# Gates and branches of a hybrid encoder with the tokens stationary and 512 columns moving, and pool sums on VectorE

## The chip, the cores and the metric

The kernel runs on one core of one Trainium2 chip. The time is the device time of one execution of the whole program in microseconds (us), two layers of the encoder from input to output. Less is better. 0.2 % of it, about 1.7 us, is what a measurement of this kernel can tell from no change.

## The reference

Two layers over 256 tokens of 1024 channels, in float32. Each layer is a mixer with three branches and a gated feed-forward part:

```python
h = rmsnorm(x, norm_mix_pre[l])
proj = jnp.einsum('bsd,de->bse', h, w_in[l])           # 1024 -> 5888
qa, ka, va, pu, qc, kc, vc, gl = jnp.split(proj, splits, axis=-1)
ya = global_axial_attention(qa, ka, va, ...)           # A: 8 heads, 2 kv heads, rope
yb = pool_mixer(pu, w_pool[l], pool_scale[l])          # B: means over 2, 4, 8, 16 tokens, minus u
yc = neighbourhood_attention(qc, kc, vc, rpb[l])       # C: 8 heads, window of the token grid
z = jnp.einsum('bsnc,ncd->bsnd', ys, w_branch[l])      # three times 512 -> 1024
gates = jax.nn.sigmoid(gl + b_gate[l]).reshape(B, S, N_BRANCH, D_MODEL)
mix = jnp.einsum('bsd,de->bse', jnp.sum(gates * z, axis=2), w_out[l])
x = x + rmsnorm(mix, norm_mix_post[l])
f = conv_gated_mlp(rmsnorm(x, norm_ffn_pre[l]), ...)   # w_up 1024 -> 2 x 2816, conv of 3 taps, gelu, w_down
x = x + rmsnorm(f, norm_ffn_post[l])
```

## The kernel before

**Weights.** All weights lie in DRAM as 264 chunks of 512 KB (128 x 1024 float32), 132 to a layer, in the order in which they are used. SP's queue loads them into `raw` (5 buffers). ScalarE (ACT) rounds each half of a chunk to `hi` (`split`, L156), and the rest, `lo` = `raw` - `hi`, is taken by VectorE (DVE), or by GpSimd (POOL) for each chunk whose number leaves 1 by 5 (L157). `hi` and `lo` have 6 buffers each. `feed` splits chunks ahead as buffers come free, at a priority that is put behind the other work's.

**Products.** Every product of the large projections is three matmuls, hi by hi, hi by lo and lo by hi (`mm3`, L193 to L195). `wstat` keeps the weights stationary: a 128 x 128 block of them is loaded and 256 tokens of `hT` (the normed, turned activations) move past it, so a matmul is 256 wide and its result is already turned (channels on partitions). `rows`, and the first projections (q, k, v), keep 128 tokens stationary and move 512 columns of weights; their result has tokens on partitions.

**A layer, in order.**
1. Projections k, v and q of attention A (chunks 0 to 5), and in `prep_a` their norm and rotary turn on DVE, ACT and POOL, one time for each half of the tokens, t = 0 and 1. At its end PE turns the rows, and ACT and DVE write `k2`, `klo` (L393) and `q2` (L397).
2. `pool_u`, four pieces of 128 channels for the pool branch, then eight pieces for q and k of attention C. Among the latter lie attention A's steps (`drive(att)`: `scores` L446 and L447, softmax L449 to L460, `turn` L468) and one step each of `pool_sums`, 12 additions, products and differences on POOL (L573 to L585).
3. v of attention C, 512 wide, whose rows POOL's queue copies into `vb`.
4. Gates and branches: 24 calls of `gated`, for the branches B, A and C in turn, one for each 128 channels d. Each is 12 matmuls of `w_branch` by `y` and 24 of the gate's columns of `w_in`, all 256 wide, into the two halves of one PSUM bank; ACT takes the tanh of the gate with its bias from `bg` (one bias per partition), DVE weighs and adds up. Attention A's end and attention C are driven between them. For branch C each call ends a merged piece, split into hi and lo, and the rows of `w_out` 0 to 2 are issued among the last calls.
5. The rest of `w_out` (`tail`), then `boundary`: `residual`, norm and the turn of `hT` for t = 0 and 1. While it runs, PE has the first two pieces of `w_up` (val and gate), with tokens stationary and 256 wide; they are turned later, in pieces f = 2 and 3.
6. The other 20 pairs of pieces of `w_up` by `wstat`, the convolution of three taps (`conv`, L749 to L751), gelu, and `w_down` three pieces behind (`LAG`), with its own tail and boundary.

**What sets the order.** Each engine runs its instructions in one order that a scheduler fixes when the program is built: it goes by the order in the code, moved by priorities (`urgent` forward, `feed` back). An engine whose next instruction waits does nothing behind it.

## Time and profile before

| | us |
|---|---|
| median of 3 runs | 850.67 (850.04 to 851.77) |
| time of the profiled execution | 851.73 |
| its span, first to last instruction | 850.0 |
| TensorE (PE) busy in it | 817.6, 96 % |
| VectorE (DVE) busy | 584.7, 69 % |
| ScalarE (ACT) busy | 505.0, 59 % |
| GpSimd (POOL) busy | 234.1, 28 % |
| mean granted clock of TensorE | 0.993 of 2.4 GHz |

The profiled execution's own time is 1.73 us over its span and 1.06 us over the median. PE's busy time counts the time from a matmul's start to its modelled end, and matmuls overlap, so the distance from start to start tells more than the duration of one. An x4 at the end of a row is a group of four instructions, and the number in brackets is the idle time before the row's first instruction, with what ended it.

### The profile page before, as it was taken

The page shows a single profiled execution, that of the slowest core. Times are in us where ns is not written, and L with a number is a line of the kernel's source. Part 1 is how long each engine was busy: PE and PEld are TensorE (multiplying, and loading weights), DVE is VectorE, ACT ScalarE, POOL GpSimd, SP SyncE. Part 2 cuts the span into 40 slices and gives each one's busy share as a digit, 9 for nine tenths or more (in the row PEclk, how much of TensorE's full clock was granted, in tenths as well). Part 3 has the DMA queues.
Part 4 walks back from the last instruction along what each step waited for, and adds up shares of the span by engine and source line. Part 5 has one row for each costly group of instructions (what it writes and reads, how often), then busy time and mean ns, then how long its engine had stood idle before and what let it go on. Part 6 is the DMA issues. An engine that isn't in the chain of part 4 may idle for free.

```text
span 850.0 us, 15776 instructions
## 1 busy us (share of the span) xinstructions
PE 817.6 (96%) x6020; PEld 762.0 (90%) x6020; DVE 584.7 (69%) x1084; ACT 505.0 (59%) x1096; POOL 234.1 (28%) x225
## 2 busy tenths in 40 slices
PE   5979999999989999999999999999998999999997
PEld 4878899999989999999988888999997999999995
DVE  4798465565688767676778975655567786676774
ACT  6467566454567656565565775654455765656562
POOL 3675321212123121212144915112122121212120
PEclk9999999999999999999999999999999999999999
DMA  7844556465465756665464555545655565566631
GB/s 272 306 155 170 162 188 209 149 203 170 150 200 170 224 175 198 175 197 175 148 198 151 173 153 170 172 152 168 195 171 165 195 184 191 177 195 181 191 99 49
DMA packets 43291, 151.44 MB, mean 178 GB/s; under 512 B 5968, under 2 KB 6224, under 8 KB 42960
## 3 DMA queue, kind: packets, MB, share of 16 engines
q1 hardware_dynamic: 42192, 148.34, 55.1%
q0 software_dynamic: 1024, 2.10, 0.8%
q8 instruction: 47, 0.77, 0.4%
q14 instruction: 28, 0.23, 0.1%
HBM read 147.27 MB, written 1.05 MB: 175 GB/s over the span
## 4 chain that ended last, share of the span: by engine, by line
PE 84%; DVE 7%; issue 3%; ACT 2%; POOL 1%; DMA 1%; SPq 0%; DVEq 0%; POOLq 0%; ACTq 0%
PE ps L193 27%; PE ps L195 26%; PE ps L194 26%; DVE lo L157 3%; POOL st L212 1%; DMA x<-in_x 1%; DVE big L239 1%; PE ps L478 1%; ACT hi L156 1%; PE ps L468 1%; PE ps L527 1%; PE ps L494 1%; PE ps L244 1%; DVE big L376 0%; DVE x L259 0%
## 5 line engine op out<-in xcount | busy, mean ns | idle before, releaser
L156 ACT ACTIVATE hi<-raw 128x512 fp32r<-128x512 f32 x528 | 315.6, 625 | 180.8 <-PE ps L194 83.6
L157 DVE TENSOR_TENSOR lo<-raw,hi 128x512 fp32r<-128x512 f32 x422 | 308.0, 746 | 115.5 <-ACT hi L156 113.3
L195 PE MATMUL ps<-hThi,lo 128*128 128x256 f32 x1216 | 345.7, 284 | 1.5 <-DVE lo L157 1.5
L193 PE MATMUL ps<-hThi,hi 128*128 128x256 f32 x1216 | 346.3, 285 | 0.0
L194 PE MATMUL ps<-hTlo,hi 128*128 128x256 f32 x1216 | 345.6, 284 | 0.0
L157 POOL TENSOR_TENSOR lo<-raw,hi 128x512 fp32r<-128x512 f32 x106 | 147.5, 1411 | 503.4 <-ACT hi L156 489.5
L193 PEld LDWEIGHTS ps<-hThi,hi 128*128 128x128 f32 x1216 | 234.8, 193 | 2.1 <-issue 0.8
L195 PEld LDWEIGHTS ps<-hThi,lo 128*128 128x128 f32 x1216 | 234.8, 193 | 1.7 <-DVE lo L157 1.7
L194 PEld LDWEIGHTS ps<-hTlo,hi 128*128 128x128 f32 x1216 | 234.7, 193 | 1.3
L749 ACT ACTIVATE w<-ps,cvp 128x256 f32<-128x256 f32 x88 | 48.6, 556 | 38.6 <-DVE w L751 38.6
L193 PE MATMUL ps<-hi,y 128*128 128x512 f32 x176 | 69.1, 393 | 0.1
L194 PE MATMUL ps<-lo,y 128*128 128x512 f32 x176 | 68.9, 392 | 0.0
L195 PE MATMUL ps<-hi,y 128*128 128x512 f32 x176 | 68.5, 389 | 0.0
L750 DVE SCALAR_TENSOR_TENSOR w<-ps,cvp,w 128x255 f32<-128x255 f32 x88 | 42.1, 480 | 34.0 <-ACT w L749 33.8
L193 PE MATMUL ps<-y,hi 128*128 128x256 f32 x192 | 55.8, 290 | 0.0
L195 PE MATMUL ps<-hi,hTlo 128*128 128x256 f32 (+1 forms) x160 | 53.2, 334 | 1.8 <-DVE hTlo L201 1.8
L193 PE MATMUL ps<-hi,hThi 128*128 128x256 f32 (+1 forms) x160 | 54.1, 341 | 0.5 <-ACT hThi L200 0.3
L195 PE MATMUL ps<-y,lo 128*128 128x256 f32 x192 | 54.3, 283 | 0.0
L194 PE MATMUL ps<-y,hi 128*128 128x256 f32 x192 | 54.3, 283 | 0.0
L194 PE MATMUL ps<-lo,hThi 128*128 128x256 f32 (+1 forms) x160 | 53.0, 333 | 0.3 <-POOL lo L157 0.3
L212 POOL TENSOR_TENSOR st<-st,mhalf 128x1 f32<-128x1 f32 (+1 forms) x20 | 20.3, 1013 | 82.6 <-DVE st L222 65.0
L751 DVE SCALAR_TENSOR_TENSOR w<-ps,cvp,w 128x255 f32<-128x255 f32 x88 | 41.9, 479 | 1.0
...
## 6 DMA issues: line engine op xcount, KB each, us to landing
raw<-in_wall SPq DMA_DIRECT2D x264, 512.0 KB, 3.8
...
```

The source lines that it names most:

```text
L156: act.activation(hi[c][:, z], raw[c][:, z], AF.Copy)
L157: (pool if c % PN == 1 else dve).tensor_tensor(lo[c][:, z], raw[c][:, z], hi[c][:, z], op=OP.subtract)
L193: pe.matmul(o, a[0], b[0], start=first, stop=False)
L194: pe.matmul(o, a[0], b[1], start=False, stop=False)
L195: pe.matmul(o, a[1], b[0], start=False, stop=last)
L212: pool.tensor_tensor(r, v, mhalf[:, :width], op=OP.pow)
L239: par["xn"] = dve.scalar_tensor_tensor(xn[:, c], xs[t][:, c], r, g[:, c], op0=OP.mult, op1=OP.mult)
L244: pe.transpose(p[:, 128 * k:128 * k + 128], xn[:, 512 * h + 128 * k:512 * h + 128 * k + 128], ident)
L468: pe.transpose(p3[:, k, t * 128:(t + 1) * 128], e[:, t, k * 128:(k + 1) * 128], ident)
L749: act.activation(u[:, c:c + S], p[:, c:c + S], AF.Identity, bias=cvp[:, l, j, 3:4], scale=cvp[:, l, j, 1:2])
L750: dve.scalar_tensor_tensor(u[:, c + 1:c + S], p[:, c:c + S - 1], cvp[:, l, j, 0:1], u[:, c + 1:c + S], op0=OP.mult, op1=OP.add)
L751: dve.scalar_tensor_tensor(u[:, c:c + S - 1], p[:, c + 1:c + S], cvp[:, l, j, 2:3], u[:, c:c + S - 1], op0=OP.mult, op1=OP.add)
```

## The change

Four things are changed.

- Gates and branches become six steps (i, c) in a layer: a branch i and a half c of its 1024 output channels. A step has 24 matmuls of `w_branch` for each half of the tokens and 48 of the gate's columns, all with tokens stationary and 512 wide, into two `pz` and two `pg` banks. The gate's bias now lies along the row, so it is a tile of its own, `gb`, spread over the partitions by a DMA on SP's queue (12 in the program, two buffers) and added by DVE before the tanh (`weighed`). The merged rows have tokens on partitions and are turned by PE (`turn_merged`, four groups of four transposes in a layer) before ACT and DVE split them. `w_out`'s first rows are issued within the last step, its rows 1 and 2 behind it.
- `pool_sums` runs on DVE in place of POOL.
- The lo of the chunks of `w_in` with columns below 2816 (q, k, v, pool, attention C) is always taken by DVE, so POOL has 44 chunks in place of 53.
- The first four pieces of `w_up`, val and gate, are 512 wide with tokens stationary (`turned`), and are turned in pieces f = 4 to 7; `w_down` follows five pieces behind. The tiles `w1` have 4 buffers in place of 6.

A "..." stands for lines left out.

```diff
 NY = 20
-TAIL_O, TAIL_D, LAG = 5, 6, 3
+TAIL_O, TAIL_D, LAG = 5, 6, 5
...
-                    out.append(("w_branch", l, i, 0, 4, 128 * d, 256))
-                wide("w_in", 0, 2816 + 1024 * i + 128 * d, 128)
-                if i == 2 and 1 <= d <= 8 - TAIL_O:
-                    out.append(("w_out", l, 0, d - 1, 1, 0, 1024))
+            for c in range(2):
+                for k in (0, 2):
+                    out.append(("w_branch", l, i, k, 2, 512 * c, 512))
+                if i == 2 and c == 1:
+                    out.append(("w_out", l, 0, 0, 1, 0, 1024))
+                wide("w_in", 0, 2816 + 1024 * i + 512 * c, 512)
+        for d in range(1, 8 - TAIL_O):
+            out.append(("w_out", l, 0, d, 1, 0, 1024))
         for d in range(8 - TAIL_O, 8):
             out.append(("w_out", l, 0, d, 1, 0, 1024))
-        wide("w_up", 0, 0, 256)
-        wide("w_up", 0, 128 * NF, 256)
-        for f in range(2, NF):
+        wide("w_up", 0, 0, 128 * NT)
+        wide("w_up", 0, 128 * NF, 128 * NT)
+        for f in range(NT, NF):
             wide("w_up", 0, 128 * f, 128)
             wide("w_up", 0, 128 * (NF + f), 128)
             if 0 <= f - LAG < NF - TAIL_D:
...
-        return sb.tile([128, 256], FT, name="w1", bufs=6)
+        return sb.tile([128, 256], FT, name="w1", bufs=4)
...
-        (pool if c % PN == 1 else dve).tensor_tensor(lo[c][:, z], raw[c][:, z], hi[c][:, z], op=OP.subtract)
+
+        lean = c % PN == 1 and (CHUNKS[c][0] != "w_in" or CHUNKS[c][5] >= 2816)
+        (pool if lean else dve).tensor_tensor(lo[c][:, z], raw[c][:, z], hi[c][:, z], op=OP.subtract)
...
-            pool.tensor_tensor(a[:, :, :271], u[:, :, :271], u[:, :, 1:272], op=OP.add)
-            pool.tensor_tensor(b[:, 1:, :269], a[:, 1:, :269], a[:, 1:, 2:271], op=OP.add)
+            dve.tensor_tensor(a[:, :, :271], u[:, :, :271], u[:, :, 1:272], op=OP.add)
+            dve.tensor_tensor(b[:, 1:, :269], a[:, 1:, :269], a[:, 1:, 2:271], op=OP.add)
...
-                pool.tensor_tensor(d, src[:, g, 8 - w // 2:264 - w // 2], invc[:, g], op=OP.mult)
-                pool.tensor_tensor(d, d, u[:, g, 8:264], op=OP.subtract)
+                dve.tensor_tensor(d, src[:, g, 8 - w // 2:264 - w // 2], invc[:, g], op=OP.mult)
+                dve.tensor_tensor(d, d, u[:, g, 8:264], op=OP.subtract)
...
-        acc = [sb.tile([128, 4, S], FT, name="q2", bufs=2) for _ in range(2)]
+        acc = [sb.tile([128, D], FT, name="q2", bufs=2) for _ in range(2)]
...
-        def gated(i, d, y, wz):
-            p = psbank()
-            for c in range(4):
-                mm3(p[:, :S], [wz[z][:, c, 128 * (d % 2):128 * (d % 2) + 128] for z in range(2)], y[c], c == 0, c == 3)
-            if d % 2 == 1:
-                done()
-            wstat(p[:, S:], "w_in")
-            g = w1()
-            act.activation(g, p[:, S:], AF.Tanh, bias=bg[:, l, 8 * i + d:8 * i + d + 1], scale=0.5)
-            a = acc[d // 4][:, d % 4]
-            if i == 1:
-                dve.scalar_tensor_tensor(a, g, 1.0, p[:, :S], op0=OP.add, op1=OP.mult)
-                return
-            m = w1()
-            dve.scalar_tensor_tensor(m, g, 1.0, p[:, :S], op0=OP.add, op1=OP.mult)
-            if i == 0:
-                dve.tensor_tensor(a, a, m, op=OP.add)
-                return
-            dve.tensor_tensor(m, a, m, op=OP.add)
...
-            merged[d] = merged["hi"][:, d], merged["lo"][:, d % 4]
-            act.activation(merged[d][0], m, AF.Copy, scale=0.5)
-            dve.scalar_tensor_tensor(merged[d][1], m, 0.5, merged[d][0].bitcast(FT), op0=OP.mult, op1=OP.subtract)
...
-        for i, y in ((1, yB), (0, yA), (2, yC)):
-            if i == 2:
...
+        def out_rows(d):
+
+            (w,) = take("w_out")
+            for t in range(2):
+                for h in range(2):
+                    rows(ob[t][h], merged[d], t, w, h, d == 0, False)
+            done()
+            feed()
+        def gate_bias(n):
+            i, c = steps[n]
+            g = sb.tile([128, 512], FT, name="gb", bufs=2)
+            nc.sync.dma_start(g, brow(bgate[l, i, 512 * c:512 * c + 512], 512))
+            gbias[n] = g
+        def weighed(i, c, t, pz, pg, gb):
+
+            g, a = w2(), acc[t][:, 512 * c:512 * c + 512]
+            dve.tensor_tensor(g, pg, gb, op=OP.add)
+            act.activation(g, g, AF.Tanh, scale=0.5)
+            if i == 1:
+                dve.scalar_tensor_tensor(a, g, 1.0, pz, op0=OP.add, op1=OP.mult)
+                return
+            dve.scalar_tensor_tensor(g, g, 1.0, pz, op0=OP.add, op1=OP.mult)
+            dve.tensor_tensor(a, a, g, op=OP.add)
...
+        def turn_merged(c, t):
+            p = psbank()
+            for k in range(4):
+                pe.transpose(p[:, 128 * k:128 * k + 128], acc[t][:, 512 * c + 128 * k:512 * c + 128 * k + 128], ident)
...
+            ts = slice(t * 128, (t + 1) * 128)
+            split_from(merged["hi"][:, 4 * c:4 * c + 4, ts], merged["lo", c][:, :, ts], p.rearrange("p (k n) -> p k n", k=4), 0.5)
...
+        steps = [(i, c) for i in (1, 0, 2) for c in range(2)]
...
+        for n, (i, c) in enumerate(steps):
+            if i == 2 and c == 0:
...
+            ws = take("w_branch", 2)
+            pz, pg = [psbank(), psbank()], []
+            for t in range(2):
+                for k in range(4):
+                    w = ws[k // 2]
+                    mm3(pz[t], [y[:, t * 128:(t + 1) * 128] for y in ys[i][k]], [w[0][:, k % 2], w[1][:, k % 2]], k == 0, k == 3)
+                    if t == 1 and k % 2 == 1:
+                        done()
+                        feed()
...
+            if n + 1 < len(steps):
+                gate_bias(n + 1)
+            if i == 2 and c == 1:
+                for t in range(2):
+                    turn_merged(0, t)
+                ob = [[psbank(), psbank()] for _ in range(2)]
+                out_rows(0)
+            ws = take("w_in", 4)
+            for t in range(2):
+                pg.append(psbank())
+                for k in range(8):
+                    w = ws[k // 2]
+                    mm3(pg[t], kx(k, t), [w[0][:, k % 2], w[1][:, k % 2]], k == 0, k == 7)
+                    if t == 1 and k % 2 == 1:
+                        done()
+                        feed()
+                weighed(i, c, t, pz[t], pg[t], gbias[n])
+                if i < 2:
+                    drive(att)
+        for d in range(1, 8 - TAIL_O):
+            if d == 1:
+                turn_merged(1, 0)
+            out_rows(d)
+        turn_merged(1, 1)
...
-        ws = take("w_up", 4)
-        tb = [psbank(), psbank()]
-        tk = [w2(), w2()]
-        for t in range(2):
-            for z in range(2):
-                for k in range(8):
-                    w = ws[2 * z + k // 4]
-                    mm3(tb[t][:, S * z:S * z + S], kx(k, t), [w[0][:, k % 4], w[1][:, k % 4]], k == 0, k == 7)
-                    if k % 4 == 3 and t == 0:
-                        drive(bound[1], z * (k // 7) * 2)
-                    elif k % 4 == 3:
-                        done()
-                        if k < 7 or z == 0:
-                            feed()
-            act.activation(tk[t], tb[t], AF.Copy)
...
+        ws = []
+        tk = [big()[:, :D] for t in range(2)]
...
+        def turned(t, c):
+            z, k = c // 4, 2 * (c % 4)
+            if k == 0:
+                tb[t, z] = psbank()
             if t == 0:
-                for _ in bound[1]:
-                    pass
-        feed()
+                ws.extend(take("w_up"))
+            for i in range(2):
+                mm3(tb[t, z], kx(k + i, t), [ws[c][0][:, i], ws[c][1][:, i]], k + i == 0, k + i == 7)
+            if t == 1:
+                done()
+                feed()
+            if k == 6:
+                act.activation(tk[t][:, 512 * z:512 * z + 512], tb[t, z], AF.Copy)
+
+        for c in range(NSPL):
+            turned(0, c)
+        for _ in bound[1]:
+            pass
+        for c in range(4):
+            turned(1, c)
+        for c in range(NSPL, 8):
+            turned(0, c)
+        for c in range(4, 8):
+            turned(1, c)
...
             p = psbank()
             wstat(p[:, :S], "w_up")
             feed()
-            if f < 4:
+            if f < 2 * NT:
                 q = psbank()
                 for z in range(2):
                     for t in range(2):
-                        c = S * z + 128 * (f - 2)
+                        c = 512 * z + 128 * (f - NT)
                         pe.transpose(q[:, S * z + 128 * t:S * z + 128 * t + 128], tk[t][:, c:c + 128], ident)
-                conv(f - 2, q)
```

On DVE, these rows stand about the first scores of attention A in layer 0. `klo` and `q` are those of `prep_a`, `lo` is a chunk's split, L449 is the maximum of the first scores. First before, then the change:

```order
L157 TENSOR_TENSOR lo<-raw,hi 128x512
L397 TENSOR_TENSOR q_191<-ps,q_191 64x4x128
L157 TENSOR_TENSOR lo<-raw,hi 128x512 x4
L397 TENSOR_TENSOR q_190<-ps,q_190 64x4x128
L393 TENSOR_TENSOR klo<-ps,k_192 64x128
L157 TENSOR_TENSOR lo<-raw,hi 128x512 x2
L393 TENSOR_TENSOR klo<-ps,k_193 64x128
L397 TENSOR_TENSOR q_191<-ps,q_191 64x4x128
L157 TENSOR_TENSOR lo<-raw,hi 128x512 x2
L449 TENSOR_REDUCE st<-ps 128x2
```

```order
L160 TENSOR_TENSOR lo<-raw,hi 128x512
L400 TENSOR_TENSOR q_190<-ps,q_190 64x4x128
L160 TENSOR_TENSOR lo<-raw,hi 128x512 x7
L400 TENSOR_TENSOR q_189<-ps,q_189 64x4x128
L396 TENSOR_TENSOR klo<-ps,k_191 64x128
L576 TENSOR_TENSOR big<-big 128x4x271
L396 TENSOR_TENSOR klo<-ps,k_192 64x128
L400 TENSOR_TENSOR q_190<-ps,q_190 64x4x128
L577 TENSOR_TENSOR big<-big 128x3x269
L160 TENSOR_TENSOR lo<-raw,hi 128x512
```

Before, seven lo splits lay ahead of the last `klo`, two of them between it and the first; with the change eight lie ahead of the first and none between, and the two sums L576 and L577 of the pool branch stand ahead of the last `klo` and behind the last `q`.

On DVE, the same place in layer 1, before and with the change:

```order
L157 TENSOR_TENSOR lo<-raw,hi 128x512 x2
L397 TENSOR_TENSOR q_5262<-ps,q_5262 64x4x128
L157 TENSOR_TENSOR lo<-raw,hi 128x512 x3
L393 TENSOR_TENSOR klo<-ps,k_5263 64x128
L397 TENSOR_TENSOR q_5261<-ps,q_5261 64x4x128
L393 TENSOR_TENSOR klo<-ps,k_5264 64x128
L157 TENSOR_TENSOR lo<-raw,hi 128x512
L397 TENSOR_TENSOR q_5262<-ps,q_5262 64x4x128
```

```order
L160 TENSOR_TENSOR lo<-raw,hi 128x512 x2
L400 TENSOR_TENSOR q_4719<-ps,q_4719 64x4x128
L160 TENSOR_TENSOR lo<-raw,hi 128x512 x7
L396 TENSOR_TENSOR klo<-ps,k_4720 64x128
L576 TENSOR_TENSOR big<-big 128x4x271
L396 TENSOR_TENSOR klo<-ps,k_4721 64x128
L400 TENSOR_TENSOR q_4718<-ps,q_4718 64x4x128
L577 TENSOR_TENSOR big<-big 128x3x269
L587 TENSOR_TENSOR w_5247<-big,invc 128x256
L400 TENSOR_TENSOR q_4719<-ps,q_4719 64x4x128
```

Here the sum L576 stands between the two last `klo`, and both last `q` stand behind it, the second behind two more instructions of the pool branch.

On PE, the start of the gates of layer 0, before (`y` is the pool branch, 256 tokens moving), and then the last step of gates and branches with the change (`y` is branch C's rows, `q` are the merged rows, `vb` and `cq` their turned hi and lo; the first name behind the arrow moves):

```order
L478 MATMUL ps<-w_1105,vA 64x256
L478 MATMUL ps<-w_1153,vA 64x256
L193 MATMUL ps<-y,hi 128x256
L194 MATMUL ps<-y,hi 128x256
L195 MATMUL ps<-y,lo 128x256
```

```order
L196 MATMUL ps<-hi,y 128x512
L197 MATMUL ps<-lo,y 128x512
L198 MATMUL ps<-hi,y 128x512
L680 MATMUL ps<-ident,q_1220 128x128 x4
L680 MATMUL ps<-ident,q_1221 128x128 x4
L196 MATMUL ps<-hi,vb 128x512
L197 MATMUL ps<-lo,vb 128x512
L196 MATMUL ps<-hi,vb 128x512
L197 MATMUL ps<-lo,vb 128x512
L198 MATMUL ps<-hi,cq 128x512 x2
```

In a step the weights now move, and in the last one the turn of the merged rows (L680) and the first rows of `w_out` stand between the branch's matmuls and the gate's.

## Rows read from the trace of the kernel before

**Rows 1.** The page: busy us (share of the span) and instructions of each engine
```profile
...
PE 817.6 (96%) x6020; PEld 762.0 (90%) x6020; DVE 584.7 (69%) x1084; ACT 505.0 (59%) x1096; POOL 234.1 (28%) x225
...
```

**Rows 2.** Windows: busy time by engine, granted clock, DMA share
```profile
...
56.00:62.00 6.00, 5.47 (x33) 5.48 (x34) 5.84 (x9) 5.35 (x11) 6.00 (x6) 0.72 0.51 175
62.00:70.00 8.00, 6.84 (x56) 6.46 (x55) 7.93 (x11) 5.52 (x15) 6.48 (x6) 1.00 0.27 74
100.00:165.00 65.00, 65.00 (x619) 62.18 (x619) 35.50 (x97) 36.75 (x93) 16.41 (x23) 1.00 0.59 188
244.00:249.00 5.00, 4.09 (x21) 3.86 (x22) 3.50 (x5) 1.20 (x2) 0.30 (x1) 0.66 0.80 249
473.00:478.00 5.00, 5.00 (x31) 5.00 (x30) 4.91 (x6) 4.92 (x9) 4.92 (x5) 0.66 0.67 187
...
```

**Rows 3.** Timeline of PE in layer 0; columns are start, us, engine, instruction
```profile
...
51.71 0.28 PE L446 MATMUL ps<-k,q 128*128 128x256 f32 x1
56.52 0.39 PE L447 MATMUL ps<-klo,q 128*128 128x256 f32 x1 [4.54 <-DVE klo L393]
...
65.86 0.63 PE L468 MATMUL ps<-ident,w 128*128 128x128 f32 x4 [0.99 <-DVE w L460]
...
```

**Rows 4.** Timeline of DVE, layer 0, first attention scores
```profile
...
48.80 6.64 DVE L157 TENSOR_TENSOR lo<-raw,hi 128x512 fp32r<-128x512 f32 x4 [1.29 <-ACT hi L156]
...
```

**Rows 5.** Timeline of POOL over the same stretch
```profile
...
47.40 2.55 POOL L157 TENSOR_TENSOR lo<-raw,hi 128x512 fp32r<-128x512 f32 x2 [3.52 <-ACT hi L156]
50.73 2.22 POOL L573 TENSOR_TENSOR big<-big 128x1084 f32<-128x1084 f32 x1 [0.78 <-POOL lo L157]
...
64.11 1.06 POOL L585 TENSOR_TENSOR w<-w,big 128x256 f32<-128x256 f32 x1
...
```

**Rows 6.** Timeline of PE, layer 1, its two waits
```profile
...
451.42 0.39 PE L195 MATMUL ps<-hThi,lo 128*128 128x256 f32 x1 [1.48 <-DVE lo L157]
...
471.62 0.38 PE L447 MATMUL ps<-klo,q 128*128 128x256 f32 x1 [1.23 <-DVE klo L393]
472.34 0.39 PE L446 MATMUL ps<-k,q 128*128 128x256 f32 x1 [0.33 <-DVE q L397]
...
```

**Rows 7.** Timeline of DVE, layer 1, the same stretch
```profile
...
449.61 5.97 DVE L157 TENSOR_TENSOR lo<-raw,hi 128x512 fp32r<-128x512 f32 x8
...
467.15 4.10 DVE L157 TENSOR_TENSOR lo<-raw,hi 128x512 fp32r<-128x512 f32 x3
...
```

**Rows 8.** Timeline of PE, layer 0, the norm before w_up
```profile
...
244.91 1.97 PE L244 MATMUL ps<-ident,big 128*128 128x128 f32 x8 [1.93 <-DVE big L239]
...
```

**Rows 9.** Timeline of PE, three changes of matmul width in layer 0
```profile
...
291.16 0.40 PE L193 MATMUL ps<-hi,y 128*128 128x512 f32 x1
...
293.91 0.28 PE L193 MATMUL ps<-hThi,hi 128*128 128x256 f32 x1
...
299.66 0.40 PE L193 MATMUL ps<-hi,y 128*128 128x512 f32 x1
...
```

**Rows 10.** Timeline of PE, first and last of 31 matmuls 512 wide
```profile
...
25.14 0.39 PE L195 MATMUL ps<-hi,hTlo 128*128 128x512 f32 x1
...
31.94 0.39 PE L195 MATMUL ps<-hi,hTlo 128*128 128x512 f32 x1
...
```

**Rows 11.** Timeline of PE, four transposes between matmuls
```profile
...
73.88 0.60 PE L468 MATMUL ps<-ident,w 128*128 128x128 f32 x4
...
74.44 0.28 PE L447 MATMUL ps<-klo,q 128*128 128x256 f32 x1
...
```

**Rows 12.** Timeline of DVE, splits while POOL rests
```profile
...
428.38 1.89 DVE L157 TENSOR_TENSOR lo<-raw,hi 128x512 fp32r<-128x512 f32 x3
...
```

**Rows 13.** Groups by line and form: busy us, mean ns, idle us before
```profile
...
L157 DVE TENSOR_TENSOR lo<-raw,hi 128x512 fp32r<-128x512 f32 x422 | 308.0, 746 | 115.5 <-ACT hi L156 113.3
...
L256 DVE TENSOR_TENSOR big<-ps,gpost 128x512 f32<-128x512 f32 x16 | 11.0, 686 | 12.9 <-ACT w L220 12.9
...
L200 ACT ACTIVATE hThi<-ps 128x512 fp32r<-128x512 f32 x16 | 9.4, 595 | 4.6 <-PE ps L244 4.5
...
```

More of the change, by code (lines that the diff above doesn't have):

```diff
@@ L679, in encoder @@
+        steps = [(i, c) for i in (1, 0, 2) for c in range(2)]
+        ys = yA, yB, yC
+        gbias = {}
+        gate_bias(0)
+        for n, (i, c) in enumerate(steps):
+            if i == 2 and c == 0:
                 for _ in att:
                     pass
[L681 to L685 removed]
+            ws = take("w_branch", 2)
+            pz, pg = [psbank(), psbank()], []
+            for t in range(2):
+                for k in range(4):
+                    w = ws[k // 2]
[3 more added lines that the diff above has]
+                        feed()
@@ L686, in encoder @@
                 if i < 2:
                     drive(att)
-                if i == 2 and 1 <= d <= 8 - TAIL_O:
-                    (w,) = take("w_out")
-                    for t in range(2):
-                        for h in range(2):
-                            rows(ob[t][h], merged[d - 1], t, w, h, d == 1, False)
-                    done()
-                feed()
+            if n + 1 < len(steps):
[5 more added lines that the diff above has]
+                out_rows(0)
@@ L757, in conv @@
             split_from(gT[f][0], gT[f][1], g)
-        for f in range(2, NF):
+        for f in range(NT, NF):
             p = psbank()
```

32 lines of the change are left out of this document (11 added, 21 removed).

## The prediction

> **What bounds the kernel now.** I read the page first. PE is busy 96 % of the span, no other engine over 69 % [rows 1], so the time is PE's matmuls and what PE loses between them, and each edit is priced by what it does there. The windows then give the stages. From 100 to 165 us, the gates and branches of layer 0, PE is busy for all 65.00 us at the full clock with DVE and ACT at 35.50 and 36.75 [rows 2]: there only matmuls count. The timeline of PE gives the losses. In layer 0's first attention scores PE stands from 51.71 + 0.12 to 56.52 for `klo`, 4.7 us, and 0.99 at 65.86 [rows 3]. In the entry of layer 1 it waits 1.48, 1.23 and 0.33 [rows 6], and in layer 0's boundary 1.93 [rows 8]. Behind the three largest the granted clock falls: 0.72 over 6 us, 0.66 over 5 us twice [rows 2], which is PE at 1.2 GHz in part of them; the loss is 6 x 0.28 = 5 x 0.34 = 1.7 us at each.
>
> Why is `klo` late? DVE is in four lo splits, 6.64 us [rows 4], 1.66 each, while POOL runs its own lo splits and pool sums, from 47.40 to 65.17 [rows 5]. Where POOL rests, three splits take 1.89, 0.63 each [rows 12]. Over the run the mean is 0.746 [rows 13], that is 422 x 0.116 = 49 us more than alone. So this trace shows DVE slower beside POOL, and much slower beside its sums.
>
> **The change part by part.**
>
> *Matmuls.* A gate step has 72 matmuls 512 wide in place of 144 that are 256 wide; six steps make 432 a layer. `w_up`'s first four pieces are 96 in place of 192. Both layers: 1056 matmuls for 2112. From 293.91 to 299.66 lie 48 matmuls 256 wide, 119.8 ns each; the 12 that are 512 wide ahead of them take 229.2 [rows 9]. In a run of 31 they take 6.80 / 30 = 226.7 [rows 10]. Two for one saves 239.6 - 229.2 = 10.4 to 239.6 - 226.7 = 12.9 ns. The new runs are 24 and 48 long, nearer to the long run, and I take 12.0: 1056 x 12.0 = **-12.7** (bounds -11.0 and -13.6).
>
> *Transposes.* Merged rows are turned in four groups of four a layer, `w_up`'s tiles in four where there were two: 12 groups more. From the start of a group, 73.88, to 74.44 lie the group and one matmul of 0.12 [rows 11], so a group takes 0.44: **+5.3**.
>
> *Pool sums and lo on DVE, layer 0.* The 12 pool instructions have 4726 columns; at 0.63 for 512 [rows 12] they take DVE 5.8 us a layer. Five chunks of lo in layer 0 and four in layer 1 come over from POOL, two halves each: 6.3 and 5.0 us. Against that stands what POOL's absence gives back. By the order, DVE has seven lo, a `q` and the first `klo` from the `q` that ended at 48.80 - 1.29 = 47.5 [rows 4]. The first two lo are POOL's of 47.40 [rows 5] and run in the idle 1.29; five more from 48.80 end near 52.0, `q` (about as long as a split) at 52.6, `klo` at 52.8. PE asks at 51.83: a wait of 1.0 in place of 4.7. The sum L576 comes behind this `klo`, and the next heads don't need what is behind it. That is -3.7. The wait of 0.99 at 65.86 [rows 3] left no fall of the clock behind (1.00 from 62 to 70 [rows 2]), so I count the 1.7 of the slow clock as gone too: **-5.4**. Bounds: 0, if the DVE work moved there keeps it as full as before, and -7, if the waits of 1.0 and 0.99 also go.
>
> *The same in layer 1.* Here DVE was less late, 3 splits in 4.10 [rows 7] and not 4 in 6.64. The eight at 449.61, 0.75 each [rows 7], held PE for 1.48 at 451.42 [rows 6]; that wait should go, since POOL's work beside them goes. But L576 (1084 columns, 1.3 us) now stands between the two last `klo`, and the `q` that the first scores need stands behind both, 1.3 + 0.3 + 0.7 = 2.3 us after the first `klo`. Where PE waited 1.23 + 0.33 I expect about 2.5, and the slow clock stays. Net **-0.5** (bounds -3 if DVE has enough lead for the sum, +1.5 if it has none at all).
>
> *`w_out` within the last step.* PE turns eight, then needs their split. ACT takes 0.595 for such a rounding and DVE about 0.69 behind it [rows 13]; the second group of transposes, 0.44, and the first matmuls, which need hi alone, cover part. **+1.0** for both layers (0 to 2.5, the whole of both splits).
>
> *The boundary.* Ahead of the turn of t = 1's `hT` PE had 48 matmuls 256 wide, 48 x 0.120 = 5.76 us; by the order it has 28 that are 512 wide, 6.36. The wait of 1.93 [rows 8] shrinks by 0.6, in layer 0 alone, and the slow clock stays: **-0.6** (0 to -2.3, with the slow clock gone).
>
> *Gates at no cost.* In a step, 72 x 0.227 = 16.3 us of PE, DVE gains two additions of the bias (512 wide from PSUM, 0.686 as L256 [rows 13]), 1.4 us; the products and sums are as many columns as before. DVE has 29 of 65 us free there [rows 2]. Without that cover they would cost 12 x 1.4 = 16 us. What the weighing can still hold up is a PSUM bank for the next `pz`: 0, bounded by 0.3 a step, 3.6. The 12 loads of `gb`, 256 KB, wait on SP's queue for one of two buffers, with weight chunks queued behind them; five raw buffers and a DMA share of 0.59 [rows 2] cover that. Fewer `w1` buffers, the longer lag of `w_down` and the bias tile taken away touch nothing that PE waits for: 0.
>
> Sum: -12.7 + 5.3 - 5.4 - 0.5 + 1.0 - 0.6 = -12.9. Against the profiled execution's 851.73 that is 838.8; the median of the runs is 1.06 below it, so **837.8 us**.
>
> The Trainium skill, "TensorE: Matmul & The Clock Gate", section "Back-to-back issue gap", gives a matmul N / 2.4 + 2.5 ns. By that, 512 wide takes 215.8 and two of 256 take 218.4, a saving of 2.6 ns for a pair, 2.7 us in all and less than the transposes cost. The trace disagrees: it has 226.7 at the least and 119.8. By the rows the matmuls give -12.7 and the sum -12.9, by the rule -2.7 and -2.9.
>
> **The rivals.**
>
> *Better than forecast.* DVE without POOL beside it gets ahead in layer 1 too, and the waits of 1.48, 1.23 and 0.33 and the slow clock go, 4.7 in place of 0.5; the boundary's wait falls to about 1 us without a slow clock behind it, 2.3 in place of 0.6. Both: 831.9; one of them, about 834. For it speaks that 49 us of DVE come back over the run; against it, the order in layer 1.
>
> *No relief at the entries.* DVE is busy 5.84 of 6 us there [rows 2], and 12 and 11 us of work come to it. If that is as much as it gets back, the sum is -12.7 + 5.3 + 1.0 - 0.6 = -7.0: **843.7**.
>
> *Hand-over in the gates.* Two `pz` and two `pg` of eight banks belong to a step, and attention has its own. If PE waits 1.0 us at each of 12 steps for a bank, the sum is 12.0 worse: **849.8**, no change. Against it: the 7 us of each step in which DVE is free.
>
> *DVE becomes the bound of the entries* (slower). Moved work is 12.1 us in layer 0 and 10.8 in layer 1; the two slowed stretches shown [rows 4, 7] give back 6.64 - 4 x 0.63 = 4.1 and 4.10 - 3 x 0.63 = 2.2. If PE waits for all of the rest, 8.0 and 8.6, the time is 850.67 - 7.0 + 16.6 = **860.3**. It decides from 3.5 us a layer. Against it: PE's eight pieces of attention C, 8 x 24 x 0.12 = 23 us, lie in this stretch too, and POOL's other work there slowed DVE as well.
>
> *512 wide hardly saves anything.* Two matmuls 256 wide as one save 2.6 ns and not 12.0: -2.7 in place of -12.7, **847.8**. Rows 9 and 10 at the same clock speak against it.
>
> It is what the rule on the issue gap in the Trainium skill's "TensorE: Matmul & The Clock Gate" would make of this kernel; the trace disagrees by 11 ns at 512 and by 10.6 at 256.
>
> **How the numbers follow.** The forecast 0.50, better 0.12, no relief 0.18, hand-over 0.08, DVE the bound 0.09, little saved 0.03. The likeliest has a range of its own from its bounds, 834 to 841. The range that leaves out the last three is **830.5 to 846**. Faster by over 0.2 % (1.7 us, about what a measurement can tell) are the forecast, better, no relief and little saved: 0.83. Within 0.2 % is the hand-over: 0.08. Slower: 0.09.
>
> **What would show it.** Matmuls: rows of 512 wide in the gates 227 ns apart, PE without idle time there. Transposes: four within 0.44. Entry of layer 0: `klo` near 52.8, lo splits of 0.65 and a granted clock of 1.00 over 56 to 62. Layer 1: a wait for `q` behind L576. The last step: a wait of about half a us for `merged`. The prediction is wrong if PE's idle time in 40 to 100 us is as long as before, if the gates show PE waiting for a bank, or if the new runs are more than 229 ns apart.

## The result, and the profile after

The changed kernel takes 836.51 us in the median of four runs (835.81 to 837.28), the kernel before 851.22 beside it; the ratio is 0.983 (95 % interval 0.981 to 0.985). The forecast was 837.8 with a range of 830.5 to 846, so the time is inside, 1.3 us below the forecast. The profiled execution took 837.28 with a span of 835.5, against 851.73 and 850.0. That the total is right does not say that its terms are: the matmuls and the boundaries gave 0.9 and 1.8 us more than their terms, the entries 1.4 less, so that the total came out this near is in part luck.

On the page, PE is 11.4 us less busy and POOL 52 us less, DVE 12 us more [rows 1]:

```profile
...
PE 806.2 (96%) x5012; PEld 707.2 (85%) x5012; DVE 597.0 (71%) x1101; ACT 501.7 (60%) x1068; POOL 182.5 (22%) x183
...
```

The windows of the changed kernel (columns as in [rows 2]: PE, PEld, DVE, ACT, POOL, granted clock, DMA share, GB/s); the first is the stretch of layer 0's first attention scores:

```profile
...
47.00:72.00 25.00, 22.72 (x184) 21.41 (x183) 24.80 (x47) 21.10 (x53) 5.63 (x12) 1.00 0.64 197
56.00:62.00 6.00, 4.61 (x39) 4.43 (x39) 5.97 (x14) 4.57 (x12) 1.25 (x3) 1.00 0.48 163
100.00:165.00 65.00, 65.00 (x397) 52.85 (x397) 41.34 (x94) 35.64 (x86) 16.30 (x18) 1.00 0.63 203
234.00:239.00 5.00, 3.70 (x16) 2.25 (x17) 4.44 (x7) 1.24 (x3) 2.17 (x2) 1.00 0.56 175
462.00:467.00 5.00, 4.64 (x26) 4.67 (x27) 4.88 (x10) 4.64 (x8) 0.00 (x0) 0.66 0.17 67
...
```

DVE is busy for 24.80 of 25 us there: the wait for `klo` is shorter, but DVE is full. The clock of 56 to 62 is 1.00 where it was 0.72, that of the boundary 1.00 where it was 0.66, and that of layer 1's entry is 0.66 as before. In the gates PE is busy for all of 65 us, as before.

The timeline of PE, at the places that answer to [rows 3, 6, 8, 10], and the turn of the merged rows:

```profile
...
53.11 0.39 PE L450 MATMUL ps<-klo,q 128*128 128x256 f32 x1 [0.73 <-DVE klo L396]
...
61.34 0.63 PE L471 MATMUL ps<-ident,w 128*128 128x128 f32 x4 [1.39 <-DVE w L463]
...
103.27 0.39 PE L198 MATMUL ps<-hi,y 128*128 128x512 f32 x1
...
108.71 0.40 PE L198 MATMUL ps<-hi,hTlo 128*128 128x512 f32 x1
...
192.31 1.03 PE L680 MATMUL ps<-ident,q 128*128 128x128 f32 x8
193.73 0.50 PE L196 MATMUL ps<-hi,vb 128*128 128x512 f32 x1 [0.38 <-ACT vb L206]
...
237.41 1.21 PE L247 MATMUL ps<-ident,big 128*128 128x128 f32 x7 [1.24 <-DVE big L242]
...
460.05 0.39 PE L450 MATMUL ps<-klo,q 128*128 128x256 f32 x1 [1.43 <-DVE klo L396]
462.36 0.36 PE L449 MATMUL ps<-k,q 128*128 128x256 f32 x1 [1.92 <-DVE q L400]
...
```

In layer 0 `klo` ends a wait of 1.0 from start to start, where it was 4.7; the row counts 0.73, from the modelled end of the matmul ahead. From 103.27 to 108.71 lie 24 matmuls 512 wide, 226.7 ns each. The eight transposes and their wait take 193.73 - 192.31 = 1.42, that is 8 x 0.109 = 0.87 and 0.55 for the split. The boundary waits 1.24 where it was 1.93. Layer 1 has the wait that the order showed, for `q` behind L576, 1.92.

The timeline of DVE at the two entries:

```profile
...
47.72 4.30 DVE L160 TENSOR_TENSOR lo<-raw,hi 128x512 fp32r<-128x512 f32 x7
...
52.77 0.28 DVE L396 TENSOR_TENSOR klo<-ps,k 64x128 fp32r<-64x128 f32 x1
52.98 1.27 DVE L576 TENSOR_TENSOR big<-big 128x1084 f32<-128x1084 f32 x1
...
455.38 4.30 DVE L160 TENSOR_TENSOR lo<-raw,hi 128x512 fp32r<-128x512 f32 x7
459.71 0.28 DVE L396 TENSOR_TENSOR klo<-ps,k 64x128 fp32r<-64x128 f32 x1
459.92 1.27 DVE L576 TENSOR_TENSOR big<-big 128x1084 f32<-128x1084 f32 x1
...
461.53 0.68 DVE L400 TENSOR_TENSOR q<-ps,q 64x512 fp32r<-64x512 f32 x1
...
```

Seven lo splits take 4.30, 0.61 each, in both layers, where four took 6.64 and three 4.10 [rows 4, 7]. The `klo` that the first scores of layer 0 need starts at 52.77. In layer 1 L576 stands between `klo` and `q`, and `q` ends at 462.2.

How the difference is made up can be worked out from PE's rows: the distances from start to start less those that the same matmuls have without a wait (0.120 and 0.227 us, 0.109 for a transpose), summed over a stretch, in us. The first two kernels of the experiments stand beside it. Layer 1 starts up to 10 us earlier in the other kernels than in the one before, so for its entry each kernel's 100 us begin at the same place of the program.

| PE's loss in | before | wide parts alone | DVE parts alone | changed |
|---|---|---|---|---|
| entry of layer 0 (25 to 100) | 10.5 | 8.3 | 6.1 | 6.1 |
| boundary of layer 0 (225 to 250) | 5.0 | 3.4 | 5.4 | 3.4 |
| entry of layer 1 (425 to 525 in the kernel before) | 9.6 | 9.5 | 9.9 | 9.5 |
| boundary of layer 1 (625 to 675) | 4.1 | 3.4 | 4.2 | 3.3 |
| last gate step (175 to 200, 600 to 625) | 0.1 | 1.4 | 0.1 | 1.4 |
| whole program | 37.6 | 34.0 | 33.5 | 31.4 |

Before to changed: 6.2 of the 14.45 us come from losses, 8.3 from matmuls less transposes. The entry of layer 1 has no share in it: there waits went and others came.

### The profile page after: what moved, and what is told of

Its sections match the earlier page's. It is cut to its first block, busy times and chain, and to the rows that moved or that the text cites. A ratio compares the mean times of both kernels' runs of the same rounds, so it can differ in the third digit from the quotient of the medians.

```text
span 835.5 us, 13700 instructions
## 1 busy us (share of the span) xinstructions
PE 806.2 (96%) x5012; PEld 707.2 (85%) x5012; DVE 597.0 (71%) x1101; ACT 501.7 (60%) x1068; POOL 182.5 (22%) x183
## 3 DMA queue, kind: packets, MB, share of 16 engines
q0 software_dynamic: 1024, 2.10, 0.9%
## 4 chain that ended last, share of the span: by engine, by line
PE 81%; DVE 10%; issue 2%; ACT 2%; POOL 2%; DMA 1%; SPq 0%; DVEq 0%; POOLq 0%; ACTq 0%
PE ps L196 26%; PE ps L197 25%; PE ps L198 25%; DVE lo L160 3%; POOL st L215 2%; DVE big L242 1%; DMA x<-in_x 1%; DVE big L379 1%; PE ps L481 1%; ACT hi L157 1%; PE ps L471 1%; DVE x L262 1%; PE ps L530 1%; PE ps L497 1%; PE ps L596 0%
## 5 line engine op out<-in xcount | busy, mean ns | idle before, releaser
L196 PE MATMUL ps<-hThi,hi 128*128 128x256 f32 x768 | 219.0, 285 | 0.0
L198 PE MATMUL ps<-hThi,lo 128*128 128x256 f32 x768 | 218.1, 284 | 0.0
L197 PE MATMUL ps<-hTlo,hi 128*128 128x256 f32 x768 | 217.9, 284 | 0.0
L196 PEld LDWEIGHTS ps<-hThi,hi 128*128 128x128 f32 x768 | 147.9, 193 | 2.2 <-issue 0.8
L197 PEld LDWEIGHTS ps<-hTlo,hi 128*128 128x128 f32 x768 | 147.9, 193 | 1.4
L198 PEld LDWEIGHTS ps<-hThi,lo 128*128 128x128 f32 x768 | 147.8, 192 | 0.1
L196 PE MATMUL ps<-hi,hThi 128*128 128x512 f32 (+1 forms) x352 | 136.0, 388 | 1.2 <-ACT hi L157 0.9
L198 PE MATMUL ps<-hi,hTlo 128*128 128x512 f32 (+1 forms) x352 | 134.4, 382 | 0.9 <-DVE hTlo L204 0.9
L197 PE MATMUL ps<-lo,hThi 128*128 128x512 f32 (+1 forms) x352 | 134.6, 383 | 0.3 <-DVE lo L160 0.2
L196 PEld LDWEIGHTS ps<-hi,y 128*128 128x128 f32 x272 | 51.2, 188 | 11.0 <-issue 1.1
L198 PEld LDWEIGHTS ps<-hi,y 128*128 128x128 f32 x272 | 51.1, 188 | 11.0
```

What stands on the lines that cost most here:

```text
L196: pe.matmul(o, a[0], b[0], start=first, stop=False)
L197: pe.matmul(o, a[0], b[1], start=False, stop=False)
L198: pe.matmul(o, a[1], b[0], start=False, stop=last)
```

## The experiments

Theory: PE's matmuls pay for the wide parts, and the entries get better since DVE no longer runs beside POOL, which slowed it. Rival: DVE's amount of work, or its order, decides in the entries, and POOL has nothing to do with it.

**The wide parts alone.** POOL has the sums (all twelve instructions) and the lo splits of before.

```diff
-            dve.tensor_tensor(a[:, :, :271], u[:, :, :271], u[:, :, 1:272], op=OP.add)
+            pool.tensor_tensor(a[:, :, :271], u[:, :, :271], u[:, :, 1:272], op=OP.add)
...
-        lean = c % PN == 1 and (CHUNKS[c][0] != "w_in" or CHUNKS[c][5] >= 2816)
+        lean = c % PN == 1
```

> The changed kernel with the pool sums on POOL and the lo splits divided as before, so that only the 512-wide parts are changed. The forecast's terms leave -12.7 + 5.3 + 1.0 - 0.6 = -7.0 against the kernel before: about 844.0, and the klo wait in layer 0 stays long (3 us or more). If the entries got better by something else than the move to DVE (the wide parts, the order), the time is near that of the changed kernel, 836.5. If the matmuls save only what a gap of N / 2.4 + 2.5 ns gives, it is 853 or more.

839.52 us, 0.985 of before (0.984 to 0.987): 12.0 us less, not 7.0. PE, POOL and DVE at layer 0's first scores, PE at layer 1's, and a window there:

```profile
...
54.27 0.39 PE L450 MATMUL ps<-klo,q 128*128 128x256 f32 x1 [1.64 <-DVE klo L396]
...
62.49 0.63 PE L471 MATMUL ps<-ident,w 128*128 128x128 f32 x4 [1.39 <-DVE w L463]
...
464.43 0.38 PE L450 MATMUL ps<-klo,q 128*128 128x256 f32 x1 [1.22 <-DVE klo L396]
...
473.37 0.63 PE L471 MATMUL ps<-ident,w 128*128 128x128 f32 x4 [1.49 <-DVE w L463]
...
```

```profile
...
52.73 2.30 POOL L576 TENSOR_TENSOR big<-big 128x1084 f32<-128x1084 f32 x1 [1.90 <-issue]
...
```

```profile
...
48.81 4.37 DVE L160 TENSOR_TENSOR lo<-raw,hi 128x512 fp32r<-128x512 f32 x5 [0.88 <-ACT hi L157]
...
```

```profile
...
462.00:467.00 5.00, 3.45 (x27) 3.05 (x26) 4.77 (x7) 3.14 (x8) 4.92 (x3) 1.00 0.65 206
...
```

Layer 0's `klo` is 1.64 late and not 4.54, though POOL has its old work: the first sum starts at 52.73, not at 50.73 [rows 5], and so beside `klo` and not beside the splits ahead of it (five take 4.37). Why that sum starts later the trace doesn't show. In layer 1 the waits of before are there, 1.22 for `klo` (1.23 in [rows 6]) and 0.33 for `q` behind it, and yet the clock stays at 1.00 where it was 0.66. The trace has no slow stretch at all between the start and the end, but that is not a gain of 3 x 1.7 us. In layer 1 PE, at the full clock, comes to the first turn sooner and waits 1.49 for `w` at 473.37, where the kernel before has no such wait, and the entry loses 9.5 where it lost 9.6.

Executions of one program differ in this too. The kernel before was run 36 times beside the experiments, with a mean granted clock of 0.992 in 18 and of 0.996 in 9. The difference is 3.4 us of PE's time, two slow stretches of 1.7, but the medians, 852.07 and 851.10, are only 1.0 apart. The four executions of the kernel of wide parts show 0.996 to 0.999, so the clock need not stay up in all of them.

By the table nearly all of the 5.0 us over the forecast are 2.2 in the entry of layer 0, 2.3 in the two boundaries where 0.6 was forecast, and 0.9 of matmuls. So the wide parts also moved an entry, which no term of the forecast had.

**The DVE parts alone**, on the kernel before.

```diff
-        (pool if c % PN == 1 else dve).tensor_tensor(lo[c][:, z], raw[c][:, z], hi[c][:, z], op=OP.subtract)
+        lean = c % PN == 1 and (CHUNKS[c][0] != "w_in" or CHUNKS[c][5] >= 2816)
+        (pool if lean else dve).tensor_tensor(lo[c][:, z], raw[c][:, z], hi[c][:, z], op=OP.subtract)
-            pool.tensor_tensor(a[:, :, :271], u[:, :, :271], u[:, :, 1:272], op=OP.add)
+            dve.tensor_tensor(a[:, :, :271], u[:, :, :271], u[:, :, 1:272], op=OP.add)
...
```

> The kernel before with only the pool sums and the lo splits of the early chunks moved to DVE. In this program's order the first sum stands ahead of the needed klo in layer 0. If DVE was slowed by POOL beside it: klo near 53.0, wait 1.2 + 0.6 in place of 4.7, layer 1 -0.5, so 847.8 (846 if the slow clock goes too). If DVE was slow by itself, the sum and two more lo splits make klo later by 2.6 us a layer: 855.

847.58 us, 0.995 (0.994 to 0.996): 4.0 us less, as the theory has it; the rival's 855 is out. PE:

```profile
...
53.26 0.39 PE L448 MATMUL ps<-klo,q 128*128 128x256 f32 x1 [0.82 <-DVE klo L394]
...
```

The wait for `klo` is 0.82 where it was 4.54, with the first sum ahead of it on DVE. Layer 0 gains 4.4 in the table, layer 1 loses 0.3. The two parts gain 12.0 and 4.0 alone and 13.7 to 14.7 together: they overlap in the entry of layer 0, where either frees the same wait.

**Each half of the DVE parts taken back**, on the changed kernel. First the sums alone on POOL:

```diff
-            dve.tensor_tensor(a[:, :, :271], u[:, :, :271], u[:, :, 1:272], op=OP.add)
+            pool.tensor_tensor(a[:, :, :271], u[:, :, :271], u[:, :, 1:272], op=OP.add)
...
```

> The changed kernel with the pool sums back on POOL, the lo splits left on DVE. If POOL's sums slow DVE beside them: the lo splits behind 50.7 us take over 1 us each, klo in layer 0 comes some 2 to 3 us later, the slow clock is back: 839 to 842. If DVE's amount of work decides: 5.8 us a layer less on DVE, and no sum ahead of q in layer 1: 833 to 836.

844.10 us, 0.991 (0.990 to 0.993), 7.6 over the changed kernel. DVE, POOL and PE:

```profile
...
56.23 4.54 DVE L160 TENSOR_TENSOR lo<-raw,hi 128x512 fp32r<-128x512 f32 x4
...
63.74 1.02 DVE L463 TENSOR_TENSOR w<-w,st 128x512 f32<-128x512 f32 x1
...
461.04 7.88 DVE L160 TENSOR_TENSOR lo<-raw,hi 128x512 fp32r<-128x512 f32 x7
...
463.46 2.48 DVE L160 TENSOR_TENSOR lo<-raw,hi 128x512 fp32r<-128x512 f32 x1
...
```

```profile
...
462.84 2.55 POOL L576 TENSOR_TENSOR big<-big 128x1084 f32<-128x1084 f32 x1 [6.00 <-ACT big L571]
...
```

```profile
...
64.91 1.08 PE L471 MATMUL ps<-ident,w 128*128 128x128 f32 x4 [4.82 <-DVE w L463]
...
```

Beside POOL's sums four lo splits take 4.54, 1.1 each. In layer 0 `klo` comes as early as in the changed kernel; what is late is `w`, the first scale of the softmax, behind the splits at 63.74, and PE's first turn waits 4.82. In layer 1 PE stands 5.2 us from start to start for `klo`. There DVE's order ahead of `klo` is that of the changed kernel, two lo splits, a `q` and seven lo splits, and the seven take 7.88 where they took 4.30. The 3.6 between them are what PE waits longer. The last row is the fifth of the seven by itself: it starts at 463.46, within POOL's first sum (462.84 to 465.39), and ends at 465.94, 0.55 us behind it. The slow clock is back in layer 0.

Then the lo splits alone on POOL:

```diff
-        lean = c % PN == 1 and (CHUNKS[c][0] != "w_in" or CHUNKS[c][5] >= 2816)
+        lean = c % PN == 1
```

> The changed kernel with the lo splits divided as before, the pool sums left on DVE. If POOL slows DVE: POOL has a pair of splits at 47 to 50 us and DVE two less, so klo moves by under 1 us; 836.5 to 838. If DVE's amount of work decides: 5 to 6 us a layer less on DVE ahead of klo, 834 to 835.5.

843.16 us, 0.990 (0.989 to 0.991), 6.6 over. The expected price was too low by 5. DVE and POOL:

```profile
...
56.79 1.79 DVE L160 TENSOR_TENSOR lo<-raw,hi 128x512 fp32r<-128x512 f32 x1
58.50 1.80 DVE L579 TENSOR_TENSOR big<-big 128x530 f32<-128x530 f32 x1
...
```

```profile
...
56.59 3.14 POOL L160 TENSOR_TENSOR lo<-raw,hi 128x512 fp32r<-128x512 f32 x2 [6.36 <-ACT hi L157]
...
```

A lo split and the third sum take 1.79 and 1.80 (0.69 and 0.71 in the changed kernel), while POOL has its pair, and PE waits 3.60 for `w`. From `klo` to the first scale DVE has the same instructions in the same order as in the changed kernel. These two are 2.2 us longer, and so is PE's wait (1.39 there). Both kernels speak against the rival, against the amount and against the order: DVE has less work in them than in the changed one, in the stretches compared the same order, and is later. Each half alone is worse than both (836.5) and than neither (839.5); the changed kernel was not run on the same chip as these, but on others at 836.5 and 837.3.

**POOL's work doubled, not moved.** The changed kernel, and beside DVE's sums POOL adds as many columns into a tile that nobody reads.

```diff
+            z = sb.tile([128, 208], FT, name="shadow", bufs=1)
+            def shadow(n):
+                for _ in range(n):
+                    pool.tensor_tensor(z, u[:, 0, :208], u[:, 3, :208], op=OP.add)
...
             dve.tensor_tensor(b[:, 1:, :269], a[:, 1:, :269], a[:, 1:, 2:271], op=OP.add)
+            shadow(9)
...
```

> The changed kernel, with POOL adding in addition as many columns as the pool sums have (23 additions of 208 columns a layer) into a tile that nobody reads; the work of every other engine is the same. If POOL's running beside DVE is what slowed DVE: lo splits and sums of DVE near 1 us and more in 50 to 65 us, later scores, +3 to +6, so 839.5 to 842.5. If not: no change, 836.5.

855.37 us, 1.004 of the kernel before (1.003 to 1.006) and 19 over the changed one. The same kernel ran once more, and its trace is read:

> The same kernel as e5_shadow once more, for a trace at the usual clock. Its time was 855, 19 us over the changed kernel, four times what POOL's effect on DVE was expected to cost. If DVE beside POOL is the cause, the trace shows lo splits, sums and softmax scales of 1 us and more from 52 us on and PE waiting 8 us or more in each layer's first scores, and little elsewhere. If it is something else (the clock, loading of instructions), PE's loss lies outside 47 to 72 us and the like stretch of layer 1.

855.41 us. DVE, POOL and PE:

```profile
...
56.63 1.12 DVE L160 TENSOR_TENSOR lo<-raw,hi 128x512 fp32r<-128x512 f32 x1
57.68 1.14 DVE L586 TENSOR_TENSOR big<-big 128x530 f32<-128x530 f32 x1
...
59.89 0.69 DVE L452 TENSOR_REDUCE st<-ps 128x2 f32<-128x512 f32 x1
...
63.82 1.10 DVE L463 TENSOR_TENSOR w<-w,st 128x512 f32<-128x512 f32 x1
...
```

```profile
...
52.87 21.65 POOL L579 TENSOR_TENSOR shadow<-big 128x208 f32<-128x208 f32 x23 [8.37 <-ACT big L571]
...
```

```profile
...
65.07 1.08 PE L471 MATMUL ps<-ident,w 128*128 128x128 f32 x4 [4.72 <-DVE w L463]
...
```

The lo split at 56.63 takes 1.12 (0.69 in the changed kernel), the sum L586 1.14 (0.71), the scale L463 1.10 (0.68). The maximum at 59.89, which reads PSUM, takes 0.69 as ever. POOL's 23 additions last 21.65 us, half as long again as the sums it once had, [rows 5], and PE waits 4.72 for the first `w`. PE's loss is 49.4 against 31.4, and 14 of the 18 us lie in the two entries (9.9 where it was 3.2 from 50 to 75, 16.6 where it was 9.5 in the entry of layer 1), with three slow stretches of the clock among them where the changed kernel has one. The other 4 are spread over the program in pieces of some tenths. PE's order is the same, instruction by instruction. DVE's is not quite: in layer 0 three lo splits and six instructions of the pool branch stand between `klo` and the first scale, where the changed kernel has two and eight. Alone that is about the same work (0.6 more, 0.7 less), but it takes 10.7 us and not 7.7, so the cost is that of POOL's running. It is three times what was expected: DVE was full there already, and what it loses PE waits for.

That agrees with the Trainium skill, "SBUF — State Buffer", section "Who interferes with whom": a DVE instruction with two inputs in SBUF contends with a GpSimd instruction that reads SBUF, and one with at most one such input does not, outside the modes in which DVE uses two ports.

How much DVE loses the traces show too. In the two entries of the kernel before, all 21 lo splits that start while an addition, product or difference of POOL runs end 0.55 us behind it; with the sums back on POOL it is 16 of 17, beside the additions for nobody 14 of 15. So the split waits for the rest of POOL's instruction and then takes about its own time: 1.12 beside these additions, 1.79 beside a lo split of POOL, 2.48 beside its first sum. It is not always DVE that waits. Beside the additions for nobody the second sum, at 55.70, keeps its 1.00 us, and POOL's addition that starts at 55.93, behind it, takes 1.28 where others take 0.62.

**Can DVE's order give the rest?** Four kernels move what PE still waits for. In the first, the first sum comes behind the last `q`:

```diff
-                    dve.tensor_tensor(q2[s][z, :, cs], p[r], q2[s][r, :, cs], op=OP.subtract)
+                    par["q2"] = dve.tensor_tensor(q2[s][z, :, cs], p[r], q2[s][r, :, cs], op=OP.subtract)
...
-            dve.tensor_tensor(a[:, :, :271], u[:, :, :271], u[:, :, 1:272], op=OP.add)
+            with tc.issue_after(par["q2"].ins):
+                dve.tensor_tensor(a[:, :, :271], u[:, :, :271], u[:, :, 1:272], op=OP.add)
```

> The changed kernel with the first pool sum behind the last q of the same layer on DVE. The wait for q in layer 1, 2.19 us behind L576, falls to about 0.6: -1.6, so 834.9; if with it the slow clock of layer 1 goes, 833.2. If the sum only filled time in which DVE had nothing else, no change: 836.5.

840.62 us, 0.988 (0.986 to 0.989): slower by 4 than the changed kernel. PE and DVE in layer 1:

```profile
...
461.57 0.39 PE L449 MATMUL ps<-k,q 128*128 128x256 f32 x1 [0.33 <-DVE q L400]
...
471.88 1.08 PE L471 MATMUL ps<-ident,w 128*128 128x128 f32 x4 [3.59 <-DVE w L463]
...
```

```profile
...
467.18 0.69 DVE L452 TENSOR_REDUCE st<-ps 128x2 f32<-128x512 f32 x1
467.79 0.42 DVE L581 TENSOR_TENSOR big<-big 128x257 f32<-128x257 f32 x1
...
471.06 0.68 DVE L463 TENSOR_TENSOR w<-w,st 128x512 f32<-128x512 f32 x1
...
```

The wait for `q` fell from 1.92 to 0.33 as expected, but the sums now stand between the maximum (467.18) and the scale (471.06), and PE waits 3.59 for `w`. Neither of the two expectations had this.

In the second, `w_out`'s first rows stand behind the last step, so the gate's matmuls cover the split of the merged rows:

```diff
-                out_rows(0)
...
-        for d in range(1, 8 - TAIL_O):
+        for d in range(8 - TAIL_O):
             if d == 1:
                 turn_merged(1, 0)
             out_rows(d)
```

> The changed kernel with the first rows of w_out behind the last gate step in place of within it; the transposes stay where they are, with 48 matmuls of the gate behind them. The wait of 0.55 us for the split of the merged rows in each layer goes: -1.1, so 835.4. If the later rows then wait for the end of the weighing: +0 to +2.

836.22 us, 0.982 (0.980 to 0.983). In its trace the two waits are gone (loss in the last steps 0.1 and not 1.4), but the entry of layer 1 loses 0.5 more. Against the changed kernel's 836.51 the times don't tell it apart; 1.1 was not confirmed.

In the third, on top of it, the scores start one piece later:

```diff
-P1, A0 = 3, 1
+P1, A0 = 3, 2
```

> The changed kernel with w_out's first rows behind the last step (as in e7_rows_late) and the first scores of attention A one piece of attention C later, 24 x 0.12 = 2.9 us more of PE's work ahead of them. If DVE being full in 47 to 72 us is what PE still waits for: the waits of 1.0 and 1.5 in layer 0 go, those of 1.6 and 2.2 in layer 1 fall to about 0.9, and the slow clock there goes: -6 to -7 from 836.2, so 829.5 to 831, with up to 1 us back at the end of attention. If the waits move along with the scores: 836.

841.82 us, 0.989 (0.988 to 0.990), 4.5 over the changed kernel on the same chip. That one took 837.29, 0.984; expected of it was:

> The changed kernel itself, for a comparison on the same chip: 836.5, within 1 us.

Of the kernel with later scores, PE and DVE's window:

```profile
...
64.75 1.09 PE L469 MATMUL ps<-ident,w 128*128 128x128 f32 x4 [3.06 <-DVE w L461]
...
464.07 0.36 PE L447 MATMUL ps<-k,q 128*128 128x256 f32 x1 [0.76 <-DVE q L398]
...
475.78 1.09 PE L469 MATMUL ps<-ident,w 128*128 128x128 f32 x4 [5.01 <-DVE w L461]
...
```

```profile
...
47.00:72.00 25.00, 21.94 (x173) 21.77 (x172) 24.78 (x46) 20.20 (x49) 5.39 (x12) 0.93 0.63 220
...
```

The waits for `klo` are gone in both layers, and of layer 1's wait for `q` 0.76 is left, but the scheduler put lo splits and sums ahead of the scale, and the first turn waits 3.06 and 5.01. DVE is busy for 24.78 of 25 us, as in the changed kernel.

In the fourth, the second and the first together, with attention A's steps ahead of the splits:

```diff
             if f >= A0:
-                drive(att)
+                with urgent():
+                    drive(att)
```

> The changed kernel with w_out's first rows behind the last step (as e7_rows_late), the first pool sum behind the last q (as e6_sums_late), and attention A's maximum, exponential and scale put ahead of the lo splits and sums wherever both could run. If what PE waits for in the entries is the place of a few instructions in DVE's order, and the lo splits have a lead that can be spent: the waits for w at 59.7 us and 470.3 us go, klo stays 1.0 and 1.6 + 0.6, so 4 us less than 836.2: 832, and 830.5 if the slow clock of layer 1 goes. If DVE is simply full there, PE waits as long for the lo splits that are now later: 836.

838.96 us, 0.985 (0.983 to 0.986). PE:

```profile
...
51.81 0.39 PE L447 MATMUL ps<-k,q 128*128 128x256 f32 x1 [2.66 <-ACT k L393]
...
458.98 0.39 PE L447 MATMUL ps<-k,q 128*128 128x256 f32 x1 [1.76 <-ACT k L393]
461.52 0.58 PE L448 MATMUL ps<-klo,q 128*128 128x256 f32 x1 [2.15 <-DVE klo L394]
...
```

The waits for `w` are gone, but the priority also moved PE's scores ahead of a piece, so PE now waits 2.66 and 1.76 for `k`, and `klo` in layer 1 comes 2.15 late. This does not test the softmax alone, since DVE and PE were moved together; DVE's order without PE's was not tried. PE's loss is 33.2 where it was 31.4. In three of the four kernels a wait was taken away and came back at another place of the same stretch.

**DVE's cover in the gates.** The bias is added twice.

```diff
-            dve.tensor_tensor(g, pg, gb, op=OP.add)
+            for _ in range(2):
+                dve.tensor_tensor(g, pg, gb, op=OP.add)
```

> The changed kernel with the addition of the gate's bias done twice (same values, 24 instructions of 0.69 us more on DVE, 16.5 us in all). If the gates' DVE work lies wholly beside PE's: no change in the steps, at most 0.7 us a layer at their end, so 836.5 to 837.9. If the hand-over of banks is on the path: 0.7 to 1.4 us a step, 845 to 853.

840.23 us, 0.986 (0.985 to 0.988), 3.7 over the changed kernel for 16.5 us more on DVE. PE's only new waits:

```profile
...
195.56 0.74 PE L198 MATMUL ps<-hi,cq 128*128 128x512 f32 x2 [0.47 <-DVE cq L207]
...
214.97 0.66 PE L681 MATMUL ps<-ident,q 128*128 128x128 f32 x4 [0.47 <-DVE q L676]
...
606.76 0.73 PE L198 MATMUL ps<-hi,cq 128*128 128x512 f32 x2 [0.90 <-DVE cq L207]
...
```

All three lie in or just behind the last step, 0.47, 0.47 and 0.90, where the merged rows are split and the last half is weighed. The other ten steps show none, so no bank is late there, even with 1.4 us more on DVE in each; the price at the end was more than twice the upper figure expected.

## Why the prediction was right, and where not

- **Matmuls**: right in kind, mis-sized by 0.9. The gates' run has 226.7 ns, so a pair saves 12.9 and not 12.0: 1056 x 12.9 = 13.6 in place of 12.7. The value for long runs, the upper bound of the term, was the one to take for runs of 24. The rival that 512 wide hardly saves anything is out. (A step's 24 matmuls of `w_branch` are 12 for each half of the tokens; the 72 of the prediction have them right.)
- **Transposes**: right, 0.109 apart; twelve groups are 5.2.
- **Entry of layer 0**: -5.4 expected, -4.4 measured (10.5 to 6.1). The step is right to 0.3 us: `klo` ends at 53.05 (expected 52.8), PE waits 1.0, the slow clock is gone. What was missed is the next wait, 1.39 for the first `w` behind the sums at 61.34, where before it was 0.99: I wrote that the next heads don't need what is behind the sum, and the first scale did. So the slow clock's 1.7 us were not all a gain: PE came sooner to a scale that DVE had no sooner.
- **Entry of layer 1**: -0.5 expected, -0.1 measured, with the wait for `q` behind L576 and the slow clock both in place. The 1.48 went as worked out; the waits for `klo` and `q` are 1.43 + 1.92 = 3.35 where about 2.5 was expected.
- **`w_out` in the last step**: +1.0 expected, two waits of 0.55, so 1.1.
- **Boundary**: -0.6 expected, -1.6 and -0.8 measured. The wait in layer 0 fell by 0.7 as worked out, and the slow clock behind it went too, which stood only in the bound; with it came 0.9 more, not 1.7. This is the boundary's half of the rival "better", which by its own terms makes 836.1 and not "about 834". Layer 1's boundary I had left out.
- **Gates at no cost**: right, up to the last step. PE has no idle time from 100 to 165 us, with DVE at 41.34 of 65.
- **Who earns it**: here the working fails, though the sum holds. It gave 7.0 to the wide parts and 5.9 to the DVE parts. Alone they give 12.0 and 4.0, together 14, and on top of the wide parts the DVE parts give 2 to 3. The step that failed is that the wide parts leave the entries as they were, which the rival "no relief at the entries", 843.7, has as well. With them POOL's first sum comes 2 us later, and the entry of layer 0 loses 2.2 less without any work moved to DVE. Which of the wide parts does it, gates or `w_up`, was not tried.
- **DVE as the bound of the entries**: as a forecast of a slower kernel wrong, as a mechanism partly there. DVE is full for 25 us, and there each of the three kernels that moved DVE's or PE's order only moved the wait, and was 2.5 to 4.5 us slower for it.

Open: when the clock falls. Before, it fell in layer 1 behind waits of 1.23 and 0.33 us (the 1.48, which the prediction counts among the three ahead of a fall, lies 20 us earlier); in the profiled execution of the wide parts alone it did not after the same three. Behind the boundary's 1.93 it fell, behind 1.24 it did not. It also differs between executions of one program. What else decides was not tried, so no share of a forecast should rest on a slow stretch going or staying. Open too is whether the fourth order would pay if PE's scores stayed in place.
